# Query, key and compression-input projections with features on partitions, put together by head in DRAM

## The chip, the cores and the metric

The kernel runs on one core of a Trainium2 chip, as one program. The metric is device time in microseconds (us); lower is better. The time before is 1575.59 us, the median of three runs (1575.22 to 1575.72). A core has five engines with an instruction queue each: TensorE (PE; its weight loads are listed apart as PEld), VectorE (DVE), ScalarE (ACT), GpSimd (POOL) and SyncE (SP), which issues nearly all DMAs of this kernel. Each queue is worked off in order; an instruction that waits holds everything behind it on its engine. Line numbers (L154) are those of the kernel before.

## The reference, cut to what matters

One layer: an attention mixer with three branches and a retention mixer run side by side on the same normed input, are gated and merged, and an MLP follows. Sequence 1024, model width 1024, everything float32.

```python
h = rmsnorm(x, norm_mix)
(q, kc, vc, ks, vs, kw, vw, nsa_g, rq, rk, rv, rg, gate_a, gate_b) = split(h @ w_in, offsets)
q  = rotary(heads(q, 8, 64), positions, 16, 500000.0)      # only the first 16 of 64 dims turn
kc, ks, kw = (rotary(heads(t, 2, 64), positions, 16, 500000.0) for t in (kc, ks, kw))
vc, vs, vw = (heads(t, 2, 64) for t in (vc, vs, vw))

def compress(k, pe, w1, w2):           # k is kc or vc; windows of 32 tokens, every 16
    blk = k[cmp_idx] + pe[None, :, None, :]
    blk = blk.transpose(0, 2, 1, 3).reshape(n_cmp, G, 32 * 64)
    return silu(blk @ w1) @ w2
# attention per 128 queries: over compressed keys, over blocks picked by top-k (16 of 16 blocks: all),
# over a sliding window of 512; three softmaxes, three gates, summed
A = nsa(q, compress(kc), compress(vc), ks, vs, kw, vw, nsa_g)
B = retention(rq, rk, rv, positions) * silu(rg)
x = x + (sigmoid(gate_a) * (A @ w_proj_a) + sigmoid(gate_b) * (B @ w_proj_b)) @ w_out
x = x + square(relu(rmsnorm(x, norm_mlp) @ w_up)) @ w_down
return rmsnorm(x, norm_final)
```

`rotary` turns pairs of dims (i, i + 8) of each head by an angle that depends on the token: `x1 cos - x2 sin`, `x1 sin + x2 cos`.

## The kernel before

The normed and transposed input stands in SBUF as `bh` and `bl`: features on partitions, 8 chunks of 128, tokens along the row. Every float32 value is kept as a rounded high part and the rest as a low part, and every product is made of three matmuls (high by high, high by low, low by high), all through the helper `mm` (L154). Weights are loaded as float32 (`raw`, three tiles of 1024 columns), split by ACT into `wh` and by DVE into `wl` (L181, L182), and kept in a ring of five tiles of two feature chunks each.

The stages that matter here come after the retention mixer, in this order:

- **Keys** (`w_kva`, columns kc, vc, ks, vs, of two groups and 64 dims each). For each block `j` of 128 tokens `dense_tok` runs 8 chunks by 3 matmuls of 512 columns, with the activations as the stationary operand, so that tokens come out on partitions. `kva_post` copies the bank to SBUF (`n`, L742), rotates 16 dims per head with eight small DVE operations (`rot_nsa`, L696 to L699), doubles the columns (`twice`, L703), and registers transposes for later: `put_c` (L731, four per block, for the compression inputs `cp`) and `put_k` (L714, two per block, for the keys `KKs`). Values are split in place (`put_v`).
- **Values and gates** (`w_kvb`: kw, vw and 24 gate columns, 280 in all). The same by token blocks, with two transposes per block for the window keys `KKw`.
- **Queries** (`w_q`, 512 columns). By token blocks from the last to the first; the rotated block `n` (L872) is stored to `q_scr` in DRAM, tokens on rows (L874). Meanwhile `cmp_flow` runs the compression: per step two `prep` (L770, L771: strided reads of `cp`), six matmuls `pc`, and its weights in four tiles of 1024 columns per flow.
- **Attention**, from the last query block to the first, gate projections (`gps`) laid between its steps. `prep_q` loads two heads' tokens twice side by side (`qt`, L675), transposes four 128x128 blocks (L949) and splits the result into `QQ` and `ql` (L952, L953), the stationary operands of the scores.

TensorE's order is the order of the program text, with a list of postponed work: `later(d, fn)` runs `fn` after `d` ticks, and a matmul block of 8 chunks has four ticks. The order on the other engines is set by a planner that follows the program's order and what it reckons to be ready. A tile waits for the last user of the memory that it takes over. The two PSUM banks of tag `mm` and the two of tag `tp` are used in turn: the third block needs the first one evicted.

Of the kernel before, what the change touches and what calls it, by code (L numbers as in the profile page):

```python
# [9 lines left out]
F32 = mybir.dt.float32  # L10
# [101 lines left out]
def hybrid_block(ctx: ExitStack, tc: tile.TileContext, a: dict, out: bass.AP):  # L112
# [11 lines left out]
    q_scr = dram.tile([P, NT, 512], F32, name="q_scr")  # L124
# [99 lines left out]

    def chunk_weights(name, n, s0=0, s1=4):
        per = 2
        W = []
        for s in range(s0, s1):
            h, l = split_w(a[name][:, s * per:(s + 1) * per, :], (per, n))
            for e in range(per):  # L230
                W.append((h[:, e * n:(e + 1) * n], l[:, e * n:(e + 1) * n]))
        return W

    with ExitStack() as es:
        psA = es.enter_context(tc.tile_pool(name="psA", bufs=2, space=PSUM, reuse_waits="tile"))
        tabs = es.enter_context(tc.tile_pool(name="tabs", bufs=1, reuse_waits="tile"))
        cret = tabs.tile([P, 768], F32, name="cret")
        cosr = tabs.tile([P, NT, 64], F32, name="cosr")
        sinr = tabs.tile([P, NT, 64], F32, name="sinr")
        cosn = tabs.tile([P, NT, 8], F32, name="cosn")  # L240
        sinn = tabs.tile([P, NT, 8], F32, name="sinn")
# [4 lines left out]
        with ExitStack() as e1:  # L246
            psR = e1.enter_context(tc.tile_pool(name="psR", bufs=1, space=PSUM, reuse_waits="tile"))
            nat = e1.enter_context(tc.tile_pool(name="nat", bufs=9, reuse_waits="tile"))
# [213 lines left out]
            with tc.manual_schedule(engines=all_):  # L462
# [96 lines left out]
                for j in range(NT):  # L559
# [38 lines left out]
                    if j == 4:  # L598
                        sines(1, *ang)
                    for i in {2: (0,), 4: (3,), 6: (5,), 7: (6,)}.get(j, ()):  # L600
                        rot_ret(i, qk[i])
# [4 lines left out]
            for c in range(2):  # L606
# [18 lines left out]
                for j in range(NT):  # L625
# [14 lines left out]
                    if j == NT - 1:  # L640
                        W = chunk_weights("w_kva" if c else "w_r1a", 512)
# [22 lines left out]
        Vs = kv.tile([P, NT, 2, P], F32R, name="Vs")  # L664
        Vw = kv.tile([P, NT, 2, P], F32R, name="Vw")
# [6 lines left out]
        def load_q(qb, g):  # L672
            qt = qtp.tile([P, 4, 2, 64], F32, name="qt")
            for e in range(2):
                nc.sync.dma_start(qt[:, :, e], q_scr[:, qb, g * 256:(g + 1) * 256].rearrange("p (h d) -> p h d", h=4))  # L675
            qs[qb, g] = qt.rearrange("p h t d -> p h (t d)")

        with ExitStack() as e2:
# [4 lines left out]
            CP = [kvp.tile([P, 2, 520], F32, name=f"cp{i}") for i in range(2)]  # L683
            for c in CP:
                V.memset(c[:, :, 512:520], 0.0)
            peT = kvp.tile([P, 6, 16], F32, name="peT")
# [3 lines left out]
            def rot_nsa(x, j):  # L690
                n = x.shape[1]
                shp = [P, n, 2, 8]
                xv = x.rearrange("p n (t d) -> p n t d", t=2)
                t1 = tmp.tile([P, 8, 2, 8], F32, name="r1", tag="r1")[:, :n]
                t2 = tmp.tile([P, 8, 2, 8], F32, name="r2", tag="r2")[:, :n]
                V.tensor_mul(t1, xv, cosn[:, j, None, None, :].to_broadcast(shp))  # L696
                V.tensor_mul(t2, xv, sinn[:, j, None, None, :].to_broadcast(shp))
                V.tensor_sub(xv[:, :, 0], t1[:, :, 0], t2[:, :, 1])
                V.tensor_add(xv[:, :, 1], t1[:, :, 1], t2[:, :, 0])  # L699

            def twice(x, w, nm):
                d = tmp.tile([P, w, 2, 64], F32, name=nm, tag=nm)
                A.activation(d, x.rearrange("p (g d) -> p g d", g=w)[:, :, None, :].to_broadcast([P, w, 2, 64]),  # L703
                             AF.Copy)
                return d.rearrange("p g t d -> p g (t d)")

            def put_k(KK, x, j, d):
                xd = twice(x, 2, "kd")

                def go():  # L710
                    tp = psA.tile([P, 4, P], F32, name="tp", tag="tp")
                    js = slice(j * P, (j + 1) * P)
                    for g in range(2):
                        T.transpose(tp[:, g], xd[:, g], ident)  # L714
                    A.activation(KK[:, :, js], tp[:, :2], AF.Copy)
                    V.tensor_sub(KK[64:, :, js], tp[64:, :2], KK[64:, :, js])

                later(d, go)

            def put_v(VV, x, j):  # L720
                xv = x.rearrange("p (g d) -> p g d", g=2)
                A.activation(VV[:, j, :, :64], xv, AF.Copy)
                V.tensor_sub(VV[:, j, :, 64:], xv, VV[:, j, :, :64])

            def put_c(x, j, d):
                nd = twice(x, 4, "cd")

                def go():
                    tp = psA.tile([P, 4, P], F32, name="tp", tag="tp")
                    for u in range(4):  # L730
                        T.transpose(tp[:, u], nd[:, u], ident)  # L731
                    tv = tp.rearrange("p (u g) (s e) -> p u g s e", u=2, e=2)
                    for u in range(2):
                        ss = slice(j * 64, (j + 1) * 64)
# [1098 lines left out]
```

## Time and profile before

| | before |
|---|---|
| median of three runs | 1575.59 us (1575.22 to 1575.72) |
| the profiled execution | 1575.88 us, span 1573.5 us |
| granted TensorE clock | 0.998 of full speed |
| keys, values, queries, attention | 234.5 to 282.75, to 313, to 369, to about 742 us |
| DMA traffic | 194 MB, mean 124 GB/s |

Busy time of an engine is the time in which at least one of its instructions ran. Matmuls overlap: a matmul's length (some 390 ns for 512 columns) is longer than the distance between two starts, so rates are read from start times. In the lists of groups the columns are the busy time and the mean length of one, and behind the second bar the idle time of the engine just before them and what ended it.

### The profile page before, as it was taken

Reading aid. Unit: us, or ns where it says so; the run is one execution under the profiler, and the core shown is the slowest. Engines: PE = TensorE matmul, PEld = TensorE weight load, DVE = VectorE, ACT = ScalarE, POOL = GpSimd, SP = SyncE. Lnnn points to the kernel's source line nnn. Section 1 sums busy time; section 2 is a strip of 40 time slices with the busy share of each in tenths; the row PEclk is TensorE's granted clock in tenths of the full one; section 3 lists DMA queues with packets and bytes.
Section 4 is the critical chain, followed back from the end, with each engine's and each line's share of the span. In section 5 each row is a group of like instructions: output and inputs, shape, how many; then the busy total and the mean of one; then the engine's idle time right before and its main releaser. Section 6 shows DMA issues by size and latency. Waiting matters only on the chain.

```text
span 1573.5 us, 22754 instructions
## 1 busy us (share of the span) xinstructions
PE 1551.0 (99%) x7905; PEld 1300.2 (83%) x7905; DVE 1053.6 (67%) x2148; ACT 736.9 (47%) x1639; POOL 512.1 (33%) x555
## 2 busy tenths in 40 slices
PE   9999999999999999999999999999999999999997
PEld 6888888987888888888888888888888888888886
DVE  6865663674777877777656278776666668786454
ACT  6653554663767766666522055222222244443352
POOL 4110010001333323333100012877776507733550
PEclk9999999999999999999999999999999999999999
DMA  6202110252111111111554341554444598574373
GB/s 210 80 18 64 58 33 25 83 172 84 35 48 35 55 48 54 42 59 60 176 165 139 128 166 57 178 175 155 152 147 147 189 357 271 189 252 131 127 255 121
DMA packets 98981, 194.35 MB, mean 124 GB/s; under 512 B 25835, under 2 KB 28147, under 8 KB 98867
## 3 DMA queue, kind: packets, MB, share of 16 engines
q1 hardware_dynamic: 98306, 191.07, 36.4%
q0 software_dynamic: 560, 1.84, 0.3%
q8 instruction: 62, 1.02, 0.3%
q14 instruction: 53, 0.43, 0.1%
HBM read 142.54 MB, written 50.33 MB: 123 GB/s over the span
## 4 chain that ended last, share of the span: by engine, by line
PE 83%; DVE 5%; issue 4%; POOL 4%; ACT 3%; DMA 1%; POOLq 0%; ACTq 0%; DVEq 0%; SPq 0%
PE mm L154 22%; PE mmu L154 21%; PE mmd L154 16%; PE gps L154 9%; PE S L154 4%; PE O L154 3%; PE pt L1059 2%; PE pt L1058 2%; ACT pW L1013 1%; DVE S L1004 1%; PE pO L154 1%; DVE pl L1061 1%; PE pc L154 1%; POOL ac L1731 1%; POOL raw L1689 1%
## 5 line engine op out<-in xcount | busy, mean ns | idle before, releaser
L1209 DVE TENSOR_TENSOR wl<-raw,wh 128x1024 fp32r<-128x1024 f32 x134 | 219.9, 1666 | 93.6 <-ACT wh L1208 92.8
L1208 ACT ACTIVATE wh<-raw 128x1024 fp32r<-128x1024 f32 x134 | 136.8, 1054 | 155.9 <-PE mmd L154 100.0
L154 PE MATMUL mm<-wh,bh 128*128 128x512 f32 (+1 forms) x448 | 174.8, 390 | 1.1 <-ACT n L742 1.0
L154 PE MATMUL mmd<-wl,wh 128*128 128x512 f32 x448 | 174.4, 389 | 0.2 <-DVE wl L1209 0.2
L154 PE MATMUL mmd<-wh 128*128 128x512 f32 x448 | 174.3, 389 | 0.0
L154 PE MATMUL mmd<-wh,wl 128*128 128x512 f32 x448 | 174.3, 389 | 0.0
L154 PE MATMUL mm<-wl,bh 128*128 128x512 f32 (+1 forms) x448 | 169.0, 377 | 0.1
L154 PE MATMUL mm<-wh,bl 128*128 128x512 f32 (+1 forms) x448 | 168.0, 378 | 0.0
L188 POOL TENSOR_SCALAR msq<-ssq 128x1 f32<-128x1 f32 (+1 forms) x32 | 7.4, 230 | 386.9 <-ACT h L194 218.5
L1061 DVE TENSOR_TENSOR pl<-pt,ph 128x512 fp32r<-128x512 f32 (+1 forms) x160 | 103.8, 649 | 31.7 <-ACT ph L1060 29.5
L1023 POOL TENSOR_SCALAR pS<-pS,cf 128x1024 f32<-128x1024 f32 (+7 forms) x64 | 47.9, 749 | 219.0 <-DVE cf L1021 67.5
L1060 ACT ACTIVATE ph<-pt 128x512 fp32r<-128x512 f32 (+1 forms) x160 | 90.5, 568 | 55.0 <-PE pt L1059 53.0
L1004 DVE CUSTOM_DVE_ANT_0 S<-S,edge_m 128x512 f32<-128x512 f32 (+3 forms) x192 | 100.7, 530 | 14.4 <-PE S L154 12.5
L154 PE MATMUL gps<-bh,wh 128*128 128x512 f32 x256 | 108.2, 423 | 0.3 <-ACT gst L912 0.2
L154 PE MATMUL mmu<-bh,wh 128*128 128x512 f32 (+1 forms) x264 | 101.0, 383 | 0.0
L154 PE MATMUL mmu<-bl,wh 128*128 128x512 f32 (+1 forms) x264 | 100.9, 383 | 0.0
L154 PE MATMUL mmu<-bh,wl 128*128 128x512 f32 (+1 forms) x264 | 100.6, 383 | 0.0
L154 PE MATMUL gps<-bh,wl 128*128 128x512 f32 x256 | 100.5, 393 | 0.0
L154 PE MATMUL gps<-bl,wh 128*128 128x512 f32 x256 | 100.5, 393 | 0.0
L154 PEld LDWEIGHTS mmd<-wl,wh 128*128 128x128 f32 x448 | 84.1, 188 | 18.1 <-DVE wl L1209 0.6
L154 PEld LDWEIGHTS mmd<-wh 128*128 128x128 f32 x448 | 84.1, 188 | 17.6
L154 PEld LDWEIGHTS mmd<-wh,wl 128*128 128x128 f32 x448 | 84.1, 188 | 17.3
(368 smaller groups left out, 4051.8 us busy)
## 6 DMA issues: line engine op xcount, KB each, us to landing
raw<-u_scr SPq DMA_DIRECT2D x56, 512.0 KB, 4.6
raw<-w_down SPq DMA_DIRECT2D x41, 512.0 KB, 5.1
raw<-w_up SPq DMA_DIRECT2D x32, 512.0 KB, 3.9
u_scr<-u SPq DMA_DIRECT2D x60, 256.0 KB, 4.2
u_scr<-s SPq DMA_DIRECT2D x45, 256.0 KB, 2.3
y<-w_down SPq DMA_DIRECT2D x16, 512.0 KB, 6.8
x<-x SPq DMA_DIRECT2D x8, 512.0 KB, 5.0
qt<-q_scr SPq DMA_DIRECT2D x32, 128.0 KB, 2.4
```

What stands on the lines that cost most here:

```text
L154: T.matmul(o, w, m, start=start, stop=stop)
L1004: V.tensor_tensor_reduce(sc, sc, mk, -0.125, BIGPOS, OP.add, OP.min, mx[:, b:b + 1])
L1013: A.activation(o, sc, AF.Exp, bias=mx[:, m:m + 1], scale=-1.0, accum_out=sums[:, b:b + 1])
L1023: G.tensor_scalar(v, v, cf[:, b:b + 1], 1.0, op0=OP.mult, op1=OP.mult)
L1058: T.transpose(tp[:, bi * 2], p0, ident)
L1059: T.transpose(tp[:, bi * 2 + 1], p1, ident)
L1060: A.activation(ph[:, :n], tp[:, :n], AF.Copy)
L1061: V.tensor_sub(pl[:, :n], tp[:, :n], ph[:, :n])
L1208: A.activation(h[:, :n], r, AF.Copy)
L1209: V.tensor_sub(l[:, :n], r, h[:, :n])
L1689: G.tensor_tensor(t, t, y12[g], op=OP.subtract)
L1731: G.tensor_tensor(t, t, x, op=OP.add)
```

## The change

Keys, the compression inputs and queries are projected with the weights as the stationary operand (`dense_feat`): a block of 128 output features by 512 tokens comes out with features on partitions, as attention wants it. Four key blocks by two token halves take the place of eight token blocks; the same for queries; the values of both kinds and the gate columns keep `dense_tok` and are made in one stage of 280 columns (`v_weights`).

The weight columns are sorted while they are split (`sorted_w`), so that all first halves of rotated dims of all heads stand in partitions 0 to 63 of one block and all second halves in 64 to 127. That block is rotated whole (`turned`), with cosine and sine tables that have features on partitions too (`trig`), made by widening the small tables on POOL and 16 transposes. The pieces of a head are then in several blocks; each is stored to its place in `k_scr` or `q_scr` (head, dim, token) by `rows` (8 partitions per DMA) and `tails` (up to 48), and a head is loaded back whole: `load_k` and `load_c` for keys and compression inputs, `load_q` for queries. The transposes of keys, compression inputs and queries are gone.

The compression input is one tile used by both flows in turn, with twice the row; it is loaded twice, the second time one token further, and read with twice the stride. The compression weights come in eight tiles of 512 columns in place of four of 1024. Retention's tables leave SBUF with retention.

```diff
+    def dense_feat(o, W, b, th):
+        for k in range(KD):
+            h, l = W[k]
+            mm(o, h[:, bs], bh[:, k, ts], k == 0, False)
+            mm(o, h[:, bs], bl[:, k, ts], False, False)
+            mm(o, l[:, bs], bh[:, k, ts], False, k == KD - 1)
+            if k % 2:
+                tick()
+    def sorted_w(is_q):
+        W = []
+        for s in range(4):
+            r = wraw.tile([P, 1024], F32, name="raw", tag="raw").rearrange("p (k c) -> p k c", k=2)
+            if is_q:
+                nc.sync.dma_start(r, a["w_q"][:, ks, :])
+            else:
+                nc.sync.dma_start(r[:, :, :P], a["w_kva"][:, ks, :P])
...
+            pairs = q_pairs if is_q else k_pairs
+            for (ho, x), (lo_, _) in zip(pairs(hv, r), pairs(lv, r)):
+                A.activation(ho, x, AF.Copy)
+                V.tensor_sub(lo_, x, ho)
...
-            kv0 = psA.tile([P, 512], F32, name="mm", tag="mm")
-            dense_tok(kv0, 0, W)
-            kv1 = psA.tile([P, 512], F32, name="mm", tag="mm")
-            dense_tok(kv1, 1, W)
+            kps = [psA.tile([P, 512], F32, name="mm", tag="mm") for _ in range(2)]
+            for th in range(2):
+                dense_feat(kps[th], W, 0, th)
             ret_z(NT - 1, 1, z7[0])
...
+            src = q_scr[g * 4:(g + 1) * 4, :, qb * P:(qb + 1) * P].rearrange("h d t -> d h t")
             for e in range(2):
+                nc.sync.dma_start(qt[e * 64:(e + 1) * 64], src)
...
+            def widen(th):
+                js = slice(4 * th, 4 * th + 4)
+                G.tensor_copy(wide[:, 0, js].rearrange("p j (v d) -> p j v d", d=8),
+                              cosn[:, js, None, :].to_broadcast([P, 4, 16, 8]))
+                for x in range(2):
+                    G.tensor_copy(wide[:, 1, js, 64 * x:64 * x + 64].rearrange("p j (v d) -> p j v d", d=8),
+                                  nsin[:, js, x, None, :].to_broadcast([P, 4, 8, 8]))
+            def turn_trig(th):
+                for i in range(2):
+                    tp = psA.tile([P, 4, P], F32, name="tp", tag="tp")
+                    for j in range(4):
+                        T.transpose(tp[:, j], wide[:, i, 4 * th + j], ident)
+                    A.activation(trig[:, i, halves(th)], tp.rearrange("p a b -> p (a b)"), AF.Copy)
+            def rows(x, dst, n):
+                for i in range(x.shape[0] // n):
+                    nc.sync.dma_start(dst[i], x[i * n:(i + 1) * n])
+            def turned(ps, th, full):
+                o = tmp.tile([P, 512], F32, name="ev", bufs=3)
+                if not full:
+                    A.activation(o, ps, AF.Copy)
+                V.tensor_mul(ra, ps, trig[:, 0, ts])
+                V.tensor_mul(rb[64:], ps[:64], trig[:64, 1, ts])
+                V.tensor_mul(rb[:64], ps[64:], trig[64:, 1, ts])
+                if full:
+                    V.tensor_add(o, ra, rb)
+                else:
+                    V.tensor_add(o[:48], ra[:48], rb[:48])
+                    V.tensor_add(o[64:112], ra[64:112], rb[64:112])
+                return o
+            def load_k(u, KK, th):
+                kf = tmp.tile([P, 2, 512], F32, name="kf", bufs=1)
+                for e in range(2):
+                    nc.sync.dma_start(kf[e * 64:(e + 1) * 64], k_scr[u, :, :, ts].rearrange("g d t -> d g t"))
+                A.activation(KK[:, :, ts], kf, AF.Copy)
+                V.tensor_sub(KK[64:, :, ts], kf[64:], KK[64:, :, ts])
+            def load_c(i):
+                CP[i] = kvp.tile([P, 2, 1088], F32, name="cp", tag="cp")
+                G.memset(CP[i][:, :, 1023:1040], 0.0)
+                src = k_scr[(0, 3)[i]].rearrange("g d t -> d g t")
+                nc.sync.dma_start(CP[i][:64, :, :S], src)
+                nc.sync.dma_start(CP[i][64:, :, :S - 1], src[:, :, 1:])
...
+            for th in range(2):
+                post_k(0, kps[th], th)
+            widen(0)
+            widen(1)
+            turn_trig(0)
+            later(2, lambda: turn_trig(1))
+            for b in (3, 1, 2):
+                for th in range(2):
+                    unit(b, th, post_k)
+                    if b == 1:
+                        later(3, lambda th=th: load_k(1, KKs, th))
+                if b == 3:
+                    later(3, lambda: load_c(0))
...
+            later(CD, lambda: chain(flow0, 1))
+            for i, (b, th) in enumerate(((0, 1), (0, 0), (1, 1), (1, 0), (2, 1), (3, 1), (2, 0), (3, 0))):
                 if i == 2:
-                    later(2, lambda: chain(cmp_flow(1), 1))
+                    load_c(1)
+                    later(5, lambda: chain(cmp_flow(1), 1))
+                unit(b, th, post_q)
+                if i == 5:
+                    later(2, lambda: load_q(7, 0))
+                    later(3, lambda: load_q(7, 1))
...
         def prep_q(qb, g):
-            tp = psT.tile([P, 4, P], F32, name="pt", tag="pt")
-            for h in range(4):
-                T.transpose(tp[:, h], qs[qb, g][:, h], ident)
+            qt = qs[qb, g]
-            A.activation(QQ, tp, AF.Copy)
-            V.tensor_sub(ql, tp, QQ)
+            A.activation(QQ, qt, AF.Copy)
+            V.tensor_sub(ql, qt, QQ)
```

More of the change, by code (lines that the diff above doesn't have):

```diff
@@ new lines, in v_weights @@
+    def v_weights():
+        W = []
+        for k0, n in ((0, 3), (3, 3), (6, 2)):
+            r = wraw.tile([P, 1024], F32, name="raw", tag="raw")[:, :n * 280]
+            rv = r.rearrange("p (k c) -> p k c", k=n)
+            nc.sync.dma_start(rv[:, :, :P], a["w_kva"][:, k0:k0 + n, 3 * P:])
+            nc.sync.dma_start(rv[:, :, P:], a["w_kvb"][:, k0:k0 + n, P:])
+            h, l = new_slot()
+            A.activation(h[:, :n * 280], r, AF.Copy)
+            V.tensor_sub(l[:, :n * 280], r, h[:, :n * 280])
+            W += [(h[:, e * 280:(e + 1) * 280], l[:, e * 280:(e + 1) * 280]) for e in range(n)]
+        return W
@@ L682, in hybrid_block @@
             tmp = e2.enter_context(tc.tile_pool(name="tmp2", bufs=2, reuse_waits="tile"))
[L683 to L686, printed above, removed]
+            CP = {}
+            peT = kvp.tile([P, 8, 16], F32, name="peT")
             nc.sync.dma_start(peT[:, 0], a["cmp_pos_k"])
             nc.sync.dma_start(peT[:, 1], a["cmp_pos_v"])
[L690 to L699, printed above, removed]
@@ L720, in put_v @@
[L720 to L734, printed above, removed]
-                        A.activation(CP[u][:64, :, ss], tv[:64, u, :, :, 0], AF.Copy)
-                        V.tensor_copy(CP[u][64:, :, ss], tv[64:, u, :, :, 1])
-                later(d, go)
@@ new lines, in plain, with tails, post_k @@
+            def plain(ps):
+                o = tmp.tile([P, 512], F32, name="ev", bufs=3)
+                A.activation(o, ps, AF.Copy)
+                return o
+            def tails(o, r0, dst, ts):
+                r, end = r0, r0 + o.shape[0]
+                while r < end:
+                    v, d = divmod(r, 48)
+                    n = min(48 - d, end - r)
+                    nc.sync.dma_start(dst(v)[16 + d:16 + d + n, ts], o[r - r0:r - r0 + n])
+                    r += n
+            def post_k(b, ps, th):
+                ts = halves(th)
+                if b == 3:
+                    o = turned(ps, th, False)
+                    for x in range(2):
+                        dst = k_scr[:3, :, 8 * x:8 * x + 8, ts].rearrange("u g d t -> (u g) d t")
+                        rows(o[64 * x:64 * x + 48], dst, 8)
+                        d0 = 32 + 16 * x
+                        nc.sync.dma_start(k_scr[3, 1, d0:d0 + 16, ts], o[64 * x + 48:64 * x + 64])
+                    return
+                o = plain(ps)
+                tails(o if b < 2 else o[:32], b * P, lambda v: k_scr[v // 2, v % 2], ts)
+                if b == 2:
+                    nc.sync.dma_start(k_scr[3, 0, :, ts], o[32:96])
+                    nc.sync.dma_start(k_scr[3, 1, :32, ts], o[96:])
```

158 lines of the change are left out of this document (86 added, 72 removed).

## The prediction, made before the changed kernel was run

> **What bounds the kernel now.** I began with the page: busy shares, then the shares of the chain that ended last.
>
> ```profile
> span 1573.5 us, 22754 instructions
> PE 1551.0 (99%) x7905; PEld 1300.2 (83%) x7905; DVE 1053.6 (67%) x2148; ACT 736.9 (47%) x1639; POOL 512.1 (33%) x555
> PE 83%; DVE 5%; issue 4%; POOL 4%; ACT 3%; DMA 1%; POOLq 0%; ACTq 0%; DVEq 0%; SPq 0%
> ```
>
> TensorE is busy almost throughout and holds 83% of the chain, so a change pays for what it takes from TensorE's own queue, and loses where it makes that queue wait. Next I cut the span at the stages the change touches: keys and values (from 234.5 us), values and gates (282.75), queries with the compression (313), attention (369 to 742). The columns are length, then busy time of PE, weight loads, DVE, ACT, POOL, then clock and DMA.
>
> ```profile
> 234.50:282.75 48.25, 47.29 (x236) 38.96 (x234) 19.46 (x97) 21.21 (x60) 1.38 (x4) 1.00 0.09 26
> 282.75:313.00 30.25, 29.09 (x223) 28.52 (x221) 17.59 (x73) 19.51 (x56) 0.00 (x0) 1.00 0.25 87
> 313.00:369.00 56.00, 56.00 (x307) 48.18 (x306) 31.66 (x82) 29.24 (x56) 0.49 (x4) 1.00 0.47 149
> 369.00:742.00 373.00, 364.88 (x2262) 312.81 (x2261) 275.41 (x945) 254.41 (x730) 117.98 (x235) 1.00 0.17 50
> ```
>
> Every stage is TensorE's: 1.0, 1.2, 0 and 8.1 us idle; no other engine is above 74%. The list of TensorE's waits from 180 to 372 us has two rows, and the attention stage's two main ones are these:
>
> ```profile
> PE tp L731 <- ACT cd L703: 1.2, 1, 1.2
> PE mm L154 <- ACT n L742: 1.0, 1, 1.0
> ...
> PE pt L1059 <- POOL pS L1023: 4.1, 6, 1.8
> PE S L154 <- ACT pS L1013: 2.2, 4, 1.0
> PE pt L949 <- DVE pl L1061: 0.7, 1, 0.7
> ```
>
> **Transposes: the large term.** The groups by shape count those that go: 32 for keys (L714), 32 for the compressed inputs (L731), 64 for queries (L949), 128 in all. The change adds 16 for its cosine and sine tables, so 112 go.
>
> ```profile
> L949 PE MATMUL pt<-ident,qt 128*128 128x128 f32 x64 | 9.6, 273 | 0.7 <-DVE pl L1061 0.7
> L714 PE MATMUL tp<-ident,kd 128*128 128x128 f32 x32 | 5.9, 272 | 0.0
> L731 PE MATMUL tp<-ident,cd 128*128 128x128 f32 x32 | 4.7, 274 | 1.2 <-ACT cd L703 1.2
> ```
>
> The 272 ns is the length of one from issue to end; neighbours overlap. What one takes from the queue must come from start times (timeline of TensorE: start, length).
>
> ```profile
> 246.35 0.39 PE L154 MATMUL mm<-wh,bl 128*128 128x512 f32 x1
> ...
> 249.09 0.39 PE L154 MATMUL mm<-wh,bl 128*128 128x512 f32 x1
> 249.32 1.03 PE L731 MATMUL tp<-ident,cd 128*128 128x128 f32 x8
> 250.11 0.48 PE L154 MATMUL mm<-wh,bh 128*128 128x512 f32 x1
> 250.43 0.40 PE L154 MATMUL mm<-wl,bh 128*128 128x512 f32 x1
> ```
>
> Twelve matmuls start between 246.35 and 249.09, so one takes 0.228 us. From 249.09 to 250.43 is 1.34 us for two of them and eight transposes: (1.34 - 0.456) / 8 = 0.11 us each, the slow start behind them included. Then 112 x 0.11 = **12.3 us** go, 5.3 of it (48 net) before attention and 7.0 (64) in it.
>
> The Trainium skill, page "TensorE: Matmul & The Clock Gate", section "Part 4: PE-mode transpose", gives about 275 ns for a 128x128 transpose inside a kernel. The trace has that figure as the length of one (272) but 0.11 us as its share of the queue; by the page's figure the saving would be 112 x 0.275 = 31 us, which I keep as a rival.
>
> **The matmuls stay.** Keys were 8 token blocks of 24 matmuls of 512 columns and become 4 feature blocks by 2 token halves of 24 such matmuls; queries likewise; values keep 8 x 24 of 280. Weights stand now where activations stood. The gates already run in that order: 24 take 5.46 us, 0.2275 each, like the 54 of the queries. I take 0.
>
> ```profile
> 356.68 12.36 PE mm L154 x54
> 369.03 5.46 PE gps L154 x24
> ```
>
> **Waits that go.** The 1.2 us wait stood before a transpose that is no more. The 1.0 us wait (the third block needs the first one's PSUM bank, evicted only behind the last retention block's copy) falls into the 0.9 us of the eight table transposes now placed there. With the 0.7 us before L949 that is **-2.9 us** (bounds -2.9 and 0).
>
> **The tables.** Six POOL copies widen cosine and sine, TensorE turns them, ACT copies them out. POOL stands idle from 240.13 on, and the memory set it did there goes into the same pool of tiles:
>
> ```profile
> 240.13 0.31 POOL L830 MEMSET Vc<- 64x256 f32 x1
> 243.72 0.38 PE L382 MATMUL pZ<-ident,z 128*128 128x128 f32 x2
> 244.14 0.38 ACT L384 ACTIVATE bt<-pZ 128x256 f32<-128x256 f32 x1 [5.40 <-PE pZ L382]
> L270 POOL TENSOR_SCALAR num<-ang 128x512 f32<-128x512 f32 x1 | 0.6, 622 | 0.1
> b_scr<-bt SPq DMA_DIRECT2D x3, 128.0 KB, 2.1
> ```
>
> Six copies of at most 0.62 us from 240.4 end at 244.1, the first half at 242.3; TensorE comes for the first half at 243.9. I take 0. If the tile's memory came free only with the last retention block (copy at 244.14, store landing 2.1 us later at 246.6), the first half would be ready at 248.5: +4.6 us is the other end. The rotation itself, four or five DVE passes of 0.69 us a block, twice for keys, is in place of small operations; with 19.46 of 48.25 us busy DVE covers it, and without that cover it is 3.5 us a block.
>
> **The sorted weights.** Each of the four key tiles is loaded by 4 DMAs and split by 5 pairs of strided operations in place of one; queries by 3 pairs. In the old kernel the last key tile was split at
>
> ```profile
> 231.51 1.04 ACT L181 ACTIVATE wh<-raw 128x1024 fp32r<-128x1024 f32 x1
> 233.50 1.22 DVE L182 TENSOR_TENSOR wl<-raw,wh 128x1024 fp32r<-128x1024 f32 x1
> ```
>
> and is wanted only 18 matmuls and a retention block into the stage, near 239. ACT took 0.38 us for 256 columns (at 244.14) and 1.04 for 1024, so 0.16 us of each does not hang on its width; four more a tile cost some 0.2 us each on ACT and on DVE, 1.6 us in all: covered by 4 us. But the last retention operations stand behind them; I take +0.5 (0 to 1.6). The wait between keys and values was ACT held in order by a split that waited for its load; values and query weights can repeat it: +1.0 (0 to 2.5).
>
> **SyncE and the gathers.** The DMA queue is the part with new work: 48 stores of keys, 52 of queries (8 before), 12 gathers back, 16 and 6 weight loads where 4 and 4 were, 16 loads of compression weights where 8 were. A rotated query half issues 16 stores at once, a rotated key half 14.
>
> ```profile
> 322.16 0.33 SPq L874 DMA_DIRECT2D q_scr<-n  x1
> 327.15 1.54 SPq L675 DMA_DIRECT2D qt<-q_scr  x3
> L675 SPq DMA_DIRECT2D qt<-q_scr x32: 359/426/768, 325.9 to 711.7; - x32
> raw<-cmp_k_w SPq DMA_DIRECT2D x4, 512.0 KB, 4.1
> q_scr<-n SPq DMA_DIRECT2D x8, 256.0 KB, 2.0
> ```
>
> Issues follow each other at 0.33 to 0.43 us, so a burst holds the queue for 16 x 0.33 = 5.3 to 6.9 us. A gather waits for its stores to land (2.0) with all later DMAs behind it. For keys nothing near waits: their gathers are wanted only in attention, the compressed keys' late in the value stage, some 20 us on. In the query stage it is narrower. There each quarter block carries a compression step:
>
> ```profile
> 312.86 1.39 PE mm L154 x6
> 314.25 0.71 PE pc L154 x6
> L770 ACT ACTIVATE xh<-cp,peT 128x128 fp32r<-128x128 f32 x32 | 15.8, 542 | 3.7 <-PE pc L154 3.6
> L771 DVE SCALAR_TENSOR_TENSOR xl<-cp,peT,xh 128x128 fp32r<-128x128 f32 x32 | 14.0, 465 | 1.8 <-ACT xh L770 1.7
> L953 DVE TENSOR_TENSOR ql<-pt,QQ x16: 676/692/693, 375.6 to 743.0; 128x512 fp32r<-128x512 f32 x16
> ```
>
> One step is 2.10 us. DVE now owes it two xl of 0.47 and a half-size weight split (half of 1.22): 1.5 us; a rotated block adds four passes of 0.69, 2.8 us, in one piece behind which a step's operands wait: about 0.6 us late, once or twice. The first burst (from about 10 us into the stage) can stand before the load of the last weight piece: issued 5 us late it lands at 18, is split at 19.4, wanted at 18.2: 1.2 us. Together **+2.0** (0 to 6). The single gathered input tile for the values is loaded when the first compression has read the last of the keys, at about 17 us, lands 4.1 to 5 us later and is wanted at 24: +0.5 for the chance that it falls behind the second burst (0 to 4).
>
> The Trainium skill, page "DMA: Bandwidth & Descriptors", section "Bandwidth", asks for transfers of 1 MiB and calls those below 64 KB dominated by a fixed cost, near 2 us; the stores here are 16 to 96 KB. The trace has the 2 us as landing time, but issues overlap it (three in 1.54 us); by the rule, one store at a time, a rival below.
>
> **Attention.** The query tile is now copied from SBUF by the same ACT and DVE operations (0.69 us on DVE); only TensorE is relieved. That stage waits 8.1 us for other engines already, so I let 1.0 of the 7.0 be lost (0 to 7.0).
>
> **The sum.** The profiled execution took 1575.9 us (2.4 around its span), 0.3 above the median of 1575.6. 1575.9 - 12.3 - 2.9 + 0.5 + 1.0 + 2.0 + 0.5 + 1.0 = 1565.7; less 0.3, **1565.4 us**.
>
> **Rivals.** (a) Forecast, 1561 to 1569: chance 0.55. (b) Late operands in the query stage at the upper ends (6 + 4 where 2.5 stand, less than covered elsewhere): 1565.4 + 7.5 = 1573 at most, 1570 in the middle; for it, DVE owes more than a step for two blocks; against it, the first steps are prepared ahead. 0.17. (c) Attention gives nothing back: its TensorE waits already name POOL, ACT and DVE, and the gap moves there: 1565.4 + 6.0 = 1571.4. Against it: DVE is 74% busy there, ACT 68%. 0.13, half of it within the bound of no change. (d) Slower: bursts ahead of loads in SyncE's queue. A load behind a burst is late by 6.9 + 4.1 us; the steps prepared ahead cover two, 4.2 us; 6.8 us of TensorE per burst. Four bursts (two of keys, two of queries); without the 2.5 already counted three of them make 1565.4 - 2.5 + 20.4 = 1583; it decides from the second uncovered burst on (1576.5). For it: the queue is in order and the bursts are new. Against: loads have three tiles ahead and key bursts come 20 us early. 0.10. (e) Stores pass singly: 52 query stores at 2.0 us are 104 us against a stage of 56, first queries 48 us late: 1613; against it stands the row with three issues in 1.54 us. 0.02. That is the DMA page's rule taken as a rate. (f) A transpose held TensorE for its whole 0.272 us: 112 x 0.272 = 30.5, so 1547; the start times speak against it. 0.03. That is the TensorE page's figure.
>
> **How the numbers follow.** No change means within 0.2%, 1572.4 to 1578.7, about what a measurement here can tell. Faster: 0.55 + 0.03 + 0.17 + 0.07 of (c) = 0.82. Same: 0.06 of (c) and 0.03 of (d), 0.09. Slower: 0.07 + 0.02 = 0.09. With every uncertain term at its best the sum is 1575.6 - 15.2 = 1560.4; the range goes from 1560 to 1573, holding (a), (b) and most of (c).
>
> **What would show it.** Right: L714, L731 and L949 gone, 16 table transposes; the key and value stages together near 73 us (78.5 now), queries 57 to 59, attention near 367, and the compression matmuls each 2.1 us apart. Wrong: a wait of 4 us at the table transposes (tables); waits of the compression matmuls on DVE or on loads above 6 us (b, d); attention still 373 (c). If the first query scores wait for their gather, the queue was the bound after all.

## The result, and the profile after

The changed kernel takes 1584.2 us, median of 4 runs (1583.1 to 1585.84), against 1575.65 (1575.22 to 1576.45) beside it: a ratio of 1.0055, 95% interval 1.0037 to 1.0072. It is slower by 8.6 us; the forecast was 1565.4, faster by 10. Line numbers from here on are those of the changed kernel, or of the experiment named.

The page of the changed kernel, span, busy shares and the shares of the chain that ended last:

```profile
span 1583.1 us, 22574 instructions
PE 1546.7 (98%) x7793; PEld 1291.3 (82%) x7793; DVE 1045.7 (66%) x2031; ACT 720.6 (46%) x1604; POOL 512.5 (32%) x565
PE 75%; DVE 8%; ACT 6%; issue 5%; POOL 5%; DMA 2%; SPq 1%; POOLq 0%; ACTq 0%; DVEq 0%
```

The profiled execution is the slowest of the four (1585.84 us). TensorE has 112 matmuls less (7905 to 7793) and 4.3 us less busy time (1551.0 before), yet the span grew by 9.6 us: TensorE stands still more, and its share of the chain fell from 83% to 75%. The stages say where. First the kernel before behind its key stage (whose row stands in the prediction), cut at the true edges: first value matmul, first query matmul, first gate projection, first projection behind attention. Then the changed kernel, key stage first. The columns are those of the prediction's second fence.

```profile
282.75:311.10 28.35, 27.19 (x214) 26.96 (x212) 15.72 (x71) 17.62 (x51) 0.00 (x0) 1.00 0.24 85
311.10:368.87 57.77, 57.77 (x316) 49.61 (x315) 33.40 (x84) 31.13 (x61) 0.49 (x4) 1.00 0.47 148
368.87:772.66 403.79, 395.15 (x2418) 337.56 (x2416) 294.51 (x1001) 273.92 (x780) 123.28 (x252) 1.00 0.18 56
```

```profile
234.57:279.31 44.74, 44.58 (x210) 36.56 (x208) 14.95 (x28) 11.91 (x27) 4.11 (x11) 1.00 0.40 100
279.31:306.94 27.63, 25.45 (x194) 24.99 (x193) 11.44 (x27) 10.65 (x29) 0.00 (x0) 1.00 0.40 116
306.94:380.00 73.06, 62.68 (x312) 52.26 (x311) 35.50 (x71) 30.96 (x66) 0.44 (x3) 0.93 0.49 134
380.00:781.81 401.81, 390.05 (x2353) 330.42 (x2352) 292.07 (x997) 273.00 (x781) 125.71 (x254) 1.00 0.18 58
```

Keys -3.5, values -0.7, queries **+15.3**, attention -2.0, the rest of the span +0.5: together +9.6. All of the loss, and more, is in the query stage, where TensorE idles 10.4 us and the granted clock is 0.93 instead of 1.00. The list of TensorE's waits from 230 to 400 us (us in all, times, longest):

```profile
PE pc L155 <- ACT w1h L876: 7.5, 2, 6.9
PE pc L155 <- DVE w1l L877: 2.7, 3, 1.2
...
PE mm L155 <- ACT gts L974: 1.2, 1, 1.2
PE mm L155 <- ACT ev L796: 1.0, 1, 1.0
```

The compression matmuls `pc` wait 10.2 us for the two parts of their weights, `w1h` and `w1l` (`gts` are the gate values and `ev` the evicted blocks, both written by ACT). ACT is only the last link. The two instructions on ACT before the long wait ends, and SyncE's queue behind them (timelines: start, length, what it waited for):

```profile
342.95 1.71 ACT L868 ACTIVATE xh<-cp,peT 128x128 fp32r<-128x128 f32 x4 [6.64 <-DMA cp<-k_scr]
344.57 1.13 ACT L876 ACTIVATE w1h<-raw 128x512 fp32r<-128x512 f32 x2
```

```profile
319.60 5.53 SPq L775 DMA_DIRECT2D q_scr<-ev  x16
325.23 0.36 SPq L163 DMA_DIRECT2D raw<-cmp_k_w  x1
329.80 5.34 SPq L775 DMA_DIRECT2D q_scr<-ev  x16
335.24 0.60 SPq L845 DMA_DIRECT2D cp<-k_scr  x1
335.88 0.60 SPq L846 DMA_DIRECT2D cp<-k_scr  x1
...
338.13 15.50 SPq L163 DMA_DIRECT2D raw<-cmp_v_w  x7
```

The second burst of 16 stores stands ahead of the two gathers of the second compression input `cp`; the last of them is issued at 335.88, ACT can read at 342.95, 7 us later, and the weight splits stand in ACT's order behind that reading. The first burst holds back the last key compression weights in the same way: they are issued at 325.23, and TensorE waits 1.23 us for them at 330.4. There is one more block, in the value stage, in the list of SyncE's waits from 270 to 312 us:

```profile
SPq L837 <- DVE gts L975: 13.5, 1, 13.5
```

```profile
291.92 1.05 ACT L838 ACTIVATE KKs<-kf 128x1024 fp32r<-128x1024 f32 x1
293.00 1.22 DVE L839 TENSOR_TENSOR KKs<-kf,KKs 64x1024 fp32r<-64x1024 f32 x1 [0.52 <-ACT KKs L838]
294.25 1.25 SPq L837 DMA_DIRECT2D kf<-k_scr  x2
```

`load_k` fills one tile, `kf`, four times. It was first filled by gathers issued at 275.3, but ACT reads it only at 291.92 (timelines of ACT, DVE and SyncE, second fence), behind the evictions of the first values, and DVE until 294.2; the `gts` that the list of waits names is DVE's next instruction. For so long the tile is not free: SyncE waits 13.5 us, until 294.25, to issue the next filling, with the query weights and the compression weights queued behind it.

And the clock: behind the wait of 6.86 us TensorE's matmuls start 0.43 us apart, not 0.23, until about 350.2 (timeline of TensorE):

```profile
345.23 0.58 PE L155 MATMUL pc<-w1h,xh 128*128 128x256 f32 x1 [6.86 <-ACT w1h L876]
...
349.75 0.61 PE L155 MATMUL mm<-bh,wh 128*128 128x512 f32 x1
350.18 0.41 PE L155 MATMUL mm<-bl,wh 128*128 128x512 f32 x1
350.43 0.39 PE L155 MATMUL mm<-bh,wl 128*128 128x512 f32 x1
```

### The profile page after: what moved, and what is told of

Same layout as the page of the kernel before. It is cut to its first block, busy times and chain, and to the rows that moved or that the text cites. A ratio compares the mean times of both kernels' runs of the same rounds, so it can differ in the third digit from the quotient of the medians.

```text
span 1583.1 us, 22574 instructions
## 1 busy us (share of the span) xinstructions
PE 1546.7 (98%) x7793; PEld 1291.3 (82%) x7793; DVE 1045.7 (66%) x2031; ACT 720.6 (46%) x1604; POOL 512.5 (32%) x565
## 4 chain that ended last, share of the span: by engine, by line
PE 75%; DVE 8%; ACT 6%; issue 5%; POOL 5%; DMA 2%; SPq 1%; POOLq 0%; ACTq 0%; DVEq 0%
PE mm L155 21%; PE mmu L155 20%; PE mmd L155 16%; PE gps L155 7%; PE S L155 3%; PE O L155 2%; ACT pW L1122 2%; PE pt L1168 2%; PE pt L1167 1%; DVE S L1113 1%; DVE pl L1170 1%; ACT pS L1122 1%; POOL pS L1132 1%; PE pO L155 1%; POOL ac L1840 1%
## 5 line engine op out<-in xcount | busy, mean ns | idle before, releaser
L155 PE MATMUL mm<-wh,bh 128*128 128x512 f32 (+1 forms) x320 | 122.5, 383 | 2.3 <-ACT gts L974 1.2
L155 PE MATMUL mm<-wl,bh 128*128 128x512 f32 (+1 forms) x320 | 118.8, 371 | 0.1
L155 PE MATMUL mm<-wh,bl 128*128 128x512 f32 (+1 forms) x320 | 118.1, 373 | 0.0
```

The source lines that it names most:

```text
L155: T.matmul(o, w, m, start=start, stop=stop)
```

## The experiments

**1. Order of the queue.** The gather of the second compression input goes ahead of the second burst of stores.

```diff
             def unit(b, th, post):
...
                 dense_feat(ps, W, b, th)
+                if (b, th, post) == (0, 0, post_q):
+                    load_c(1)
...
-                if i == 2:
-                    load_c(1)
```

> The changed kernel with one thing moved: the gather of the second compression input is issued ahead of the 16 stores of the second rotated query half instead of behind them, on the same queue. Theory (queue order): the gather waited some 8 us in SyncE's queue, first for the rotation, then behind 16 stores; moved, it is issued near 327 us, lands before TensorE wants it, the 6.9 us wait and the fall of the clock that follows it go: 1584 - 6.9 - 4 = 1573. Rival (landing): the two 512 KB gathers take 7 us to land whatever stands ahead, beside eight weight loads, and TensorE still waits 5 us or more: 1580. Rival (operands): ACT and DVE can't split the half-size compression weights in time, and the waits of the compression matmuls stay near 10 us in sum: 1582.

Measured: 1583.36 us, ratio to before 1.0039 (1.0025 to 1.0054), query stage 70.9. A row each of the timelines of SyncE and of ACT in that kernel:

```profile
329.79 8.09 SPq L775 DMA_DIRECT2D q_scr<-ev  x16
```

```profile
343.76 1.35 ACT L876 ACTIVATE w1h<-raw 128x512 fp32r<-128x512 f32 x2 [4.86 <-DMA raw<-cmp_v_w]
```

The input came in time, but the burst now took 8.1 us (0.5 per store in place of 0.33), and the next thing in the queue, the weights of the second compression (issued from 340.23), became the late one. The wait had moved by one place in the queue: the `pc` waits came to 7.6 us in place of 10.2, the longest 3.7. That the order alone cost the time was refuted.

**2. One store for a rotated block.** The block goes to DRAM as it stands, by one DMA; the gathers read a head in three pieces (six DMAs per filling of `kf` in place of two).

```diff
...
-                    for x in range(2):
-                        rows(o[64 * x:64 * x + 64], q_scr[:, 8 * x:8 * x + 8, ts], 8)
+                    nc.sync.dma_start(q_rot[:, ts], o)
...
+            def take_k(dst, e, u, cols):
+                for x in range(2):
+                    r0, p0 = 64 * x + 16 * u, 64 * e + 8 * x
+                    nc.sync.dma_start(dst[p0:p0 + 8], k_rot[r0:r0 + 16, cols].rearrange("(g f) t -> f g t", g=2))
+                nc.sync.dma_start(dst[64 * e + 16:64 * e + 64], k_scr[u, :, 16:, cols].rearrange("g d t -> d g t"))
...
```

> The changed kernel with the bursts taken away: a rotated block is stored by one DMA to a place of its own, and the gathers read each head in three pieces (6 DMAs for a query tile or key tile where 2 were). The order in the queue is kept. Theory (queue order): the second compression gather still waits for the rotation ahead of it in the queue, but not for 15 more stores; it is issued 5 us earlier than in the changed kernel, the wait falls from 6.9 to about 2 us and the clock holds: 1584 - 5 - 4 = 1575. Rival (more gathers cost): the extra gather DMAs block the queue before keys and queries and give it back: 1582 or more. Rival (operands): nothing changes, 1583.

Measured: 1582.28 us, ratio 1.004 (1.0025 to 1.0055). No burst is left, the value stage lost its two waits (24.8 us), and yet the query stage took 73.3. TensorE's main waits in it, and SyncE's timeline:

```profile
PE pc L157 <- DVE w1l L891: 5.2, 2, 4.7
PE mm L157 <- ACT wh L270: 3.7, 2, 2.8
```

```profile
304.73 0.61 SPq L840 DMA_DIRECT2D kf<-k_rot  x2
...
306.80 0.90 SPq L260 DMA_DIRECT2D raw<-w_q  x2
```

Two of the query weight loads stand behind gathers that wait for `kf`, and are issued at 306.8 us, when the query stage has run for 2.6. A second jam, `kf`, had come up behind the first, and in a heavier form: in the changed kernel, with two DMAs per filling, the last query weight load is issued at 303.05, before its query stage begins.

**3 and 4. What a transpose is worth in attention.** The kernel before without its 64 query transposes in attention, and the changed kernel with 64 put back.

```diff
-            tp = psT.tile([P, 4, P], F32, name="pt", tag="pt")
-            for h in range(4):
-                T.transpose(tp[:, h], qs[qb, g][:, h], ident)
+            tp = qs[qb, g]
```

> The kernel before with the 64 query transposes of attention left out: the query tile is copied as it was loaded, so the scores are not the reference's. It asks what these transposes are worth alone. Theory (waits move): the stage is held by ACT, DVE and POOL between TensorE's pieces, and only 2 us come back: 1574. Rival (queue time): 64 transposes take 7.0 us of a queue that is busy 98%, and 6 to 7 us come back: 1569.

> The changed kernel with the 64 query transposes put back ahead of the same copies (so the scores are not the reference's). Theory (waits move): the stage before had 5 us more of waits after the change; with the transposes back it is 2 us longer and the waits fall again: 1586. Rival (queue time): 7 us longer, 1591.

Measured: 1573.81 us without them (ratio 0.9986, 0.9977 to 0.9995); the attention stage 402.2 in place of 403.8. With them put back 1586.42 (1.0065, 1.005 to 1.008), attention 404.0 in place of 401.8. TensorE's main waits in the attention stage, of the kernel before and of the kernel before without the transposes:

```profile
PE pt L1059 <- POOL pS L1023: 4.6, 7, 1.8
PE S L154 <- ACT pS L1013: 2.2, 4, 1.0
```

```profile
PE pt L1057 <- POOL pS L1021: 6.8, 14, 1.8
PE S L154 <- ACT pS L1011: 3.2, 5, 0.9
```

TensorE reaches the same softmax results earlier and waits 14 times for POOL in place of 7. Both experiments give about 2 us for 64 transposes: in the stage rows of the changed kernel TensorE's busy time falls by 5.1 (395.15 to 390.05; 0.08 us a transpose) and its idle time grows from 8.6 to 11.8.

**5 to 9. The two jams, singly and together.** The gathers into `kf` are issued by POOL's queue in place of SyncE's: alone, with the early gather of `cp`, with both of these and the single store, and with the single store but without the early gather. The last run has the single store and the early gather with `kf` on SyncE.

```diff
-                    nc.sync.dma_start(kf[e * 64:(e + 1) * 64], k_scr[u, :, :, ts].rearrange("g d t -> d g t"))
+                    G.dma_start(kf[e * 64:(e + 1) * 64], k_scr[u, :, :, ts].rearrange("g d t -> d g t"))
```

> The changed kernel with one edit: load_k issues its gathers of the keys into kf on POOL's queue, so that SyncE no longer waits 13.5 us there (281 to 294) for the one kf tile to come free with the query weights and compression weights behind it. Theory 'the kf wait makes the query stage late': the w_q pieces load some 10 us sooner, the splits leave the query stage's start, the three waits for w1 at 312 to 319 (0.41, 0.66, 1.08 us) go, 1581 to 1582. Rival 'the 16-store bursts alone': the 6.9 us wait at 345 stays, as does the low clock behind it, 1583 to 1585. I expect the rival to keep most of the time, because the 6.9 us wait is behind the second burst of query stores and not behind kf.

> Both edits at once: the gathers into kf on POOL's queue and the gather of the second compression input ahead of the second burst of 16 query stores. If the query stage's 17 us were the sum of independent queue waits, each cured by its own edit, this gives 1577 to 1580 (the order edit alone gave 1583.4). If the weights of the second compression flow stay behind the stretched burst (they were the 4.86 us wait with the order edit alone), it stays at 1582 to 1584 with the wait at w1h near 343 us.

> All three at once: one store for a rotated block in place of 14 or 16, the gather of the second compression input early, the gathers into kf on POOL's queue. Theory 'SyncE's queue in order is what costs the query stage 17 us': no burst, no kf wait, so waits of the compression matmuls below 3 us in sum, the clock above 0.9 in each 10 us of the query stage, the stage 57 to 62 us, the time 1568 to 1572. Rival 'the stage's own operands on ACT and DVE (half-size weight splits, strided preparation, four DVE passes) are late whatever the queue does': stage above 66 us, time above 1577, and TensorE's waits there name ACT and DVE whose own waits name no DMA.

> Two of the three edits that together gave 1571.2: one store for a rotated block and the kf gathers on POOL, but the gather of the second compression input back at its place after two query blocks. It is issued some 10 us later than with the early place and lands about 7 us after that, so it should be late by 4 to 8 us for the first steps of the second flow: 1575 to 1580 with waits on xh. If without the bursts the queue reaches it in time anyway: 1571 to 1572.

> The other two of three: one store for a rotated block and the early gather, but the kf gathers on SyncE. As with one store alone the query weights load late behind the kf waits (w_q at 306.8, splits with waits of 3.7 and 4.7 us and a low clock behind them): 1578 to 1582. If kf did not matter once the rest is cured: 1571 to 1573.

Measured, with experiments 1 and 2 beside them (stage lengths and granted clock from the stage rows of each, time as median and ratio to before):

| stores of a rotated query half | `kf` issued by | gather of `cp` | query stage | clock in it | time | ratio (95%) |
|---|---|---|---|---|---|---|
| 16 | SyncE | as changed | 73.1 | 0.93 | 1584.2 | 1.0055 (1.0037 to 1.0072) |
| 16 | SyncE | early | 70.9 | 0.93 | 1583.36 | 1.0039 (1.0025 to 1.0054) |
| 16 | POOL | as changed | 73.3 | 0.91 | 1586.42 | 1.0056 (1.0041 to 1.0072) |
| 16 | POOL | early | 70.0 | 0.95 | 1582.35 | 1.0043 (1.0028 to 1.0058) |
| 1 | SyncE | as changed | 73.3 | 0.88 | 1582.28 | 1.004 (1.0025 to 1.0055) |
| 1 | SyncE | early | 74.4 | 0.91 | 1583.41 | 1.0042 (1.0028 to 1.0056) |
| 1 | POOL | early | 60.4 | 1.00 | 1571.17 | 0.9966 (0.9954 to 0.9979) |
| 1 | POOL | as changed | 60.3 | 1.00 | **1569.45** | **0.9964 (0.9951 to 0.9977)** |

Either jam left standing costs the stage about 13 us (the `kf` jam in its form with six DMAs per filling); only with both gone does it fall to 60.3. With `kf` off SyncE and the bursts left, the wait behind the second burst even grew, to 8.3 us. With 16 stores the early gather shortens the stage by 2 to 3 us, in times whose intervals overlap. With the single store it does nothing that can be told apart: the two DMAs of the second `cp` gather were issued at 321.25 and 326.32 without it and at 321.49 and 326.56 with it, because the order in which the DMAs stand in SyncE's queue came out the same. My expectation of 1575 to 1580 for the last row of the table was wrong for that reason. That row beats both kernels. Its value, query and attention stages:

```profile
279.97:304.77 24.80, 24.80 (x193) 24.80 (x192) 12.00 (x29) 11.30 (x29) 6.52 (x12) 1.00 0.41 127
304.77:365.04 60.27, 58.13 (x312) 49.34 (x311) 34.70 (x69) 29.74 (x65) 4.08 (x10) 1.00 0.58 156
365.04:766.75 401.71, 390.07 (x2354) 330.69 (x2352) 292.75 (x997) 272.82 (x781) 125.47 (x254) 1.00 0.18 58
```

TensorE idles 2.1 us in the query stage, in two waits of 1.1 for `xl` and `xh`; without them the stage would be 58.1, the 57.8 of the kernel before. So the 73 us hold no new work for TensorE, only waits and what follows from them.

**10. Half-size compression weights alone**, in the kernel before.

```diff
...
-                    return split_w(a[n1][:, s * 4:(s + 1) * 4, :], (4, 256), pool=wr2)
+                    r, _ = load_raw(a[n1][:, s * 2:(s + 1) * 2, :], (2, 256))
+                    h = wr2.tile([P, 512], F32R, name="w1h", tag="w1h")
+                    l = wr2.tile([P, 512], F32R, name="w1l", tag="w1l")
...
```

> The kernel before with one part of the change alone: the compression weights in eight tiles of 512 columns per flow in place of four of 1024. Theory 'queue': in the old query stage SyncE has room (8 stores in all), so this part alone costs nothing: 1575 to 1577. Rival 'half-size weights come too late for the compression steps wherever they are': waits of the compression matmuls on w1h or w1l of 3 us or more and 1579 or above.

Measured: 1575.6 us, ratio 0.9996 (0.9987 to 1.0005). This part is free as long as the loads come in time.

**11 and 12. Keys without queries.** The changed kernel with the query part of the kernel before (token blocks, transposes in attention); then the same with `kf` on POOL's queue.

```diff
...
-            for i, (b, th) in enumerate(((0, 1), (0, 0), (1, 1), (1, 0), (2, 1), (3, 1), (2, 0), (3, 0))):
+            for i, j in enumerate(reversed(range(NT))):
...
-                unit(b, th, post_q)
+                dense_tok(ps, j, W)
...
+                rot_nsa(n.rearrange("p (h d) -> p h d", h=8)[:, :, :16], j)
+                nc.sync.dma_start(q_scr[:, j], n)
...
```

> The change without its query part: keys and compression inputs by features as in the changed kernel (stores, gathers, kf, cp as there), queries as in the kernel before (token blocks, eight stores of 128 tokens, 64 transposes in attention). Theory 'the loss sits in the query stage's DMA traffic alone': key and value stages together 72.3 us as in the changed kernel, query stage 56 to 58, the time 1570 to 1572. Rival 'the keys' gathers and half-size weights do the harm, whatever the queries do': the query stage stays above 62 us, 1577 or more.

> The same, and the gathers into kf are issued on POOL's queue. Where the kf wait on SyncE still delays the query weights and the first compression weights in the kernel with keys alone, this is 1 to 3 us less than that: 1568 to 1570; where it does not, the two are equal.

Measured: 1575.63 us (ratio 0.9999, 0.999 to 1.0009) and 1574.13 (0.999, 0.998 to 0.9999). TensorE's waits in the first one's query stage, and that stage's row:

```profile
PE pc L155 <- DVE w1l L887: 1.4, 2, 1.1
PE pc L155 <- ACT w1h L886: 0.6, 1, 0.6
```

```profile
306.76:367.93 61.17, 58.70 (x312) 49.28 (x311) 35.34 (x87) 31.39 (x65) 0.44 (x3) 1.00 0.56 159
```

The first query matmul comes 4.3 us sooner than before (306.76 against 311.10), and the query stage gives 3.4 of it back, with eight plain query stores: what is late there are the weight splits, behind `kf`. With `kf` on POOL's queue the stage is 59.5, but the first query matmul comes at 307.81, so little is gained in all. Both theories were half right. The 13 us need the query part of the change: without it the `kf` gathers cost the query stage 1.6 us (61.2 to 59.5). But the keys alone gain nothing, because their own gathers make the next stage wait; why they gain only some 1.8 us without that wait was not looked into.

**13 and 14. Is the low clock TensorE's own doing?** The kernel before, made to stand still once in the query stage, with no DMA added: a chain of small POOL copies (the diff has the long one, 14; the short one has 4), and one transpose of their result next in TensorE's order.

```diff
                 nc.sync.dma_start(q_scr[:, j], n)
+                if i == 3:
+                    dm = tmp.tile([P, 256], F32, name="dm", tag="kd")
+                    G.tensor_copy(dm, n[:, :256])
+                    for _ in range(14):
+                        G.tensor_scalar(dm, dm, 1.0, 0.0, op0=OP.mult, op1=OP.add)
+                    tpd = psA.tile([P, 4, P], F32, name="tp", tag="tp")
+                    T.transpose(tpd[:, 0], dm[:, :P], ident)
...
```

> The kernel before, with TensorE made to stand still once, in the query stage and without any DMA: after the fourth query block five chained POOL copies of the block's 256 columns, and a transpose of the result next in TensorE's order. From 0.62 us per POOL copy of 512 columns I estimate some 0.35 us each, with the block's eviction ahead a wait of 2 to 3.5 us. Theory 'the low clock follows from TensorE's own idle time': the granted clock falls for some us behind the wait if 3 us are enough, so the time is 1578 (wait alone) to 1581 (wait and clock). Rival 'the low clock of the query stage comes from the DMA load or from slow operands': clock stays 1.00, 1578 to 1579.

> The same with fifteen chained POOL copies: a wait of 5.5 to 8 us, as long as the 6.9 us of the changed kernel. Theory 'the clock follows from idle time': matmul starts 0.43 us apart instead of 0.228 for 4 to 5 us behind the wait, the stage 10 to 13 us longer, 1585 to 1588. Rival: the wait alone, 1581 to 1584, starts 0.228 apart behind it.

Measured: 1582.13 us for a wait of 3.65 (ratio 1.0036, 1.0023 to 1.0048) and 1586.69 for one of 8.52 (1.0063, 1.0048 to 1.0078). The timelines of TensorE, of the long wait and then of the short one:

```profile
353.21 0.47 PE L881 MATMUL tp<-ident,dm 128*128 128x128 f32 x1 [8.52 <-POOL dm L879]
...
353.91 0.63 PE L154 MATMUL mm<-wl,bh 128*128 128x512 f32 x1
354.34 0.63 PE L154 MATMUL mm<-wh,bl 128*128 128x512 f32 x1
```

```profile
348.36 0.33 PE L881 MATMUL tp<-ident,dm 128*128 128x128 f32 x1 [3.65 <-POOL dm L879]
...
351.30 0.63 PE L154 MATMUL mm<-wh,bh 128*128 128x512 f32 x1
351.73 0.63 PE L154 MATMUL mm<-wl,bh 128*128 128x512 f32 x1
```

Starts 0.43 us apart with no DMA added: the low clock follows TensorE's own idle time. Behind the short wait it comes late (starts 0.23 apart until 349.7, 0.43 from then on to 353.3); behind the long one at once, from 353.2 to 356.9. The query stage is 63.3 and 68.3 us in place of 57.8, so 5.5 for a wait of 3.65 and 10.5 for one of 8.52: some 1.9 us on top of either, about half of the 3.4 and 3.6 us that TensorE then works at low clock.

## Why the prediction was wrong, step by step

**What failed first: SyncE and the gathers (+2.0, 0 to 6) and the gathered input tile (+0.5, 0 to 4).** The query stage lost 15.3 us. The prediction had the parts: the burst of 5.3 us at 0.33 a store (5.34 measured), the order of the queue, weight loads behind a burst, a `cp` that might fall behind the second one. It went wrong in three places.

- "For keys nothing near waits: their gathers are wanted only in attention". This asked when the data is wanted. It had to ask what is queued behind the waiting instruction: SyncE stood 13.5 us for the one `kf` tile, with the query and compression weights behind it. The rows of the table with one store show what such a wait can cost: 13 us of the query stage between `kf` on SyncE and on POOL, there with six DMAs per filling.
- The `cp` gather was put at a chance of +0.5 for falling behind the second burst, and at 4.1 to 5 us for landing. It fell behind it, and could be read 7 us after its issue: one wait of 6.9. With the gather moved ahead, the weights behind the burst were late instead (experiment 1), so it was the burst that cost, whichever load stood behind it.
- Nothing was reckoned for the clock. Of the stage's 15.3 us the listed waits are 10.2; two stretches of low clock (319.5 to 322.9 and 345.2 to 350.2) at starts 0.43 in place of 0.228 apart make some 3.9; about 1.2 is not accounted for.

**Rival (d)**, bursts ahead of loads, at 1583 and a chance of 0.10, is the one that came nearest. Its mechanism was there, but its sum came out near by other terms: not three uncovered bursts at 6.8 us, but one wait of 6.9, smaller waits from the bursts and `kf`, and the clock. The reason against it, "loads have three tiles ahead and key bursts come 20 us early", left out that a queue in order can be held by a wait as well as by work.

**Attention (1.0 of 7.0 lost).** 2.0 came back, as rival (c) had it (nothing, 0.13): the mechanism was named there, "the gap moves there", and experiments 3 and 4 show it in both directions. "DVE is 74% busy there, ACT 68%" was no reason against it: an average over a stage does not tell that a result comes in time, and the wait that grew was POOL's, which is 31% busy there.

**Transposes (0.11 us each, 12.3 in all).** The order of size held against rival (f): TensorE's busy time fell by 5.1 us for 64 in attention (0.08 each) and by 4.45 for 48 net in the key and value stages (0.09 each). The 0.11 held the slow start behind the transposes too; at 0.08 to 0.09 the term is 9.6.

**Waits that go (-2.9).** The key stage's 1.0 us of idle time fell to 0.2, as reckoned. The value stage has 2.2 where it had 1.2, waits on `gts` and `ev` on ACT; the prediction's +1.0 for the sorted weights named ACT held in its order. In the version with the single store both are gone (24.8 us), together with SyncE's stores ahead of the first `cp` gather; that these were the cause was not tested by itself. Keys and values together gained 4.2 us against 6.0. The "near 73 us (78.5 now)" was met by its number only: the edge at 313 lay 1.9 us inside the query stage; from edge to edge it is 76.6 to 72.4.

**Right.** The tables cost nothing: no wait stands before their transposes. The matmuls in the other orientation cost nothing: without its waits the query stage of the best version is 58.1 us against 57.8. The half-size weights by themselves cost nothing (experiment 10). The first burst, taken alone, cost what was reckoned for it (a wait of 1.23 us, 1.2 forecast). With both jams gone the steps before attention come out near the sum: 6.3 us gained to the first query matmul (6.0 forecast), 2.5 lost in the query stage (2.5 forecast). That is in part luck: the 6.3 are 4.45 for transposes and 1.9 for waits (forecast 5.3 and 2.2, less 1.5 for weights, which cost nothing there), and the 2.5 come without the bursts for which they were put down. The 1569.45 us of that version are 4.1 above the forecast, and attention's share, 2.1 in place of 6.7, makes that up (4.6; the rest of the span came out 0.4 shorter).

## What to carry to other kernels

For every DMA that a change adds, ask what it waits for and what stands behind it in its queue, not only when its data is wanted; a tile with one buffer filled several times makes the whole queue wait for its reader. A cure of one jam that changes nothing is no proof that it was harmless: here two jams in one queue hid each other, and only the pair, one store per block and the gathers on another queue, gave 13 us back. Time taken from a bound engine comes back only where the next result is early enough; count the waits in that stage before crediting it, and reckon a stall of TensorE of 3.65 us or more at its own length and about 2 us more, as these runs had it.

## What the hardware showed that I had not expected

The granted clock. A single wait of 3.65 or 8.52 us was followed by about 3.5 us in which matmuls start 0.43 us apart in place of 0.228. In the changed kernel the same came at 319.5, behind three waits of 0.41, 0.66 and 1.08 us in the 8 us ahead of it; in the kernel with keys alone, waits of 0.28, 0.56 and 1.08 us at nearly the same place had no such stretch behind them. The clock column tells them apart. In every trace the clock's changes lie whole multiples of 3.41 us apart. So TensorE's idle time can be counted in such steps: first the changed kernel, then keys alone, then the short wait of experiment 13 (columns as in the stage rows).

```profile
316.09:319.50 3.41, 1.67 (x9) 1.00 (x8) 3.27 (x6) 1.99 (x4) 0.00 (x0) 1.00 0.11 40
319.50:322.91 3.41, 3.41 (x12) 2.84 (x11) 2.65 (x6) 1.31 (x3) 0.00 (x0) 0.50 0.43 115
```

```profile
316.78:320.20 3.42, 2.07 (x11) 1.70 (x12) 3.31 (x6) 2.40 (x6) 0.00 (x0) 1.00 0.41 123
320.20:323.61 3.41, 3.41 (x22) 3.06 (x21) 2.39 (x5) 2.15 (x6) 0.00 (x0) 1.00 0.88 240
```

```profile
342.96:346.38 3.42, 1.75 (x11) 1.38 (x9) 2.74 (x10) 2.10 (x5) 0.39 (x1) 1.00 0.55 174
346.38:349.79 3.41, 1.43 (x7) 1.21 (x8) 0.00 (x0) 0.28 (x1) 1.62 (x4) 1.00 0.21 77
349.79:353.20 3.41, 3.41 (x13) 2.92 (x12) 0.00 (x0) 0.00 (x0) 0.00 (x0) 0.50 0.02 5
```

TensorE idled 1.74 us in a step and the next was at half clock; 1.35 us, and it was not; 1.67 us, and it was not, then 1.98, and it was. That is why the low clock came late behind the short wait. Counted over the sixteen traces, all 26 steps at full clock with 1.9 us of idle time or more were followed by half clock and none with less than 1.6; in between both occur. So what decides is TensorE's idle time within one step, be it one wait or several, and the limit is about half of the step. When a step at half clock is followed by another was not worked out.

The Trainium skill, page "TensorE: Matmul & The Clock Gate", section "Why this matters for your kernels", asks for no idle gaps over about 3 us between matmuls, since one window of idle time halves the clock; its section "Part 1: The HAM clock gate (the "warmup" mystery)" puts the window at about 3.4 us. The runs agree with the half rate and with the 3.4 us (the steps of 3.41 above); the stretch behind the three short waits goes beyond the rule as stated, since about half a step of idle time was enough.

Two gathers of the compression input, 64 partitions and 512 KB each, could be read 7 us after the second's issue, where the profile of before had 4.1 us for one load of 512 KB of weights; and with those gathers just ahead of them the same 16 stores took 0.5 us each to issue instead of 0.33 (experiment 1).
